# Transposing through a DMA copy, as one-pass float32r, in a four-layer decoder trunk

## The chip, the cores and the metric

The kernel runs on one core of a Trainium2 chip. The metric is device time in microseconds (us) from start to end of one execution. The compute engines of a core have queues of their own and run side by side: PE (TensorE) does matrix products and transposes into PSUM, ACT (ScalarE) and DVE (VectorE) do elementwise work, POOL (GpSimd) does some elementwise work too and can issue DMAs, SP (SyncE) only issues DMAs. A profile of one execution lists the instructions of each engine, PE's loads of its stationary operand in a row of their own (PEld).

## The reference

One sequence of 256 tokens of width 1024 goes through four pre-norm residual layers, all in float32. Each layer has a token mixer (layers 0 and 3 stick-breaking attention with 8 heads, layer 1 differential attention, layer 2 a short gated convolution), a cross-attention into 256 memory tokens, an output projection, and a SwiGLU feed-forward layer with inner width 2816:

```python
mem_n = _rmsnorm(mem, g_mem)
for i in range(DEPTH):
    kind = i % N_MIXERS
    hn = _rmsnorm(x, g_mix[i])
    proj = hn @ w_in[i]                       # 1024 -> 3 * 1024 + 256
    cols, mq = proj[..., :3 * MIX_WIDTH], proj[..., 3 * MIX_WIDTH:]
    if kind == 0:
        mix = _stick_breaking(cols)
    elif kind == 1:
        mix = _diff_attention(cols, lam_q1[j], ...)
    else:
        mix = _short_conv(cols, conv_w[j])    # gate_b * conv3(gate_c * h)
    mo = _memory_attention(mq, mem_n, w_mem_kv[i])
    x = x + jnp.concatenate([mix, mo], axis=-1) @ w_o[i]
    x = x + _swiglu(_rmsnorm(x, g_ffn[i]), w_ffn_in[i], w_ffn_out[i])
return _rmsnorm(x, g_final)
```

## The kernel before

**Weights.** The weights stream from HBM once. `wchunk` loads 512 KB (two blocks of 128 input channels by 512 columns, or one by 1024) into one of three `raw` buffers over SP's queue and splits it exactly in two: ACT writes the leading part `whi` (line 128), DVE the remainder `wlo` (line 129), both float32r, from a pool `wsplit` with eight buffers for each. Activations are split in the same way, and `mm3` (lines 133 to 135) makes each product of three float32r products: high by high, high by low, low by high. There are 428 chunks and 1728 such triples.

**Projections.** `proj` multiplies the 256 tokens, as two tiles of 128 (index `t`), by 512 columns: for each tile 8 blocks of input channels, so 24 products into one PSUM bank, and then an evacuation by ACT or DVE (`evac`). All four chunks of a projection are used by tile 0 and then again by tile 1, so a chunk becomes free only in the second tile. The first projection of the kernel loads one block a chunk, eight chunks in all. `out_proj` accumulates four PSUM banks at once over all chunks of a matrix.

**Transposes.** A projection's result has tokens on the partitions; attention, the convolution and the next product need channels there. So the evacuated tile is transposed on PE, 128 by 128 at a time, against a float32 identity `ident`, into PSUM, and copied or split from there. Queries, keys and the two convolution operands go through `to_T` (line 260), the product of the SwiGLU gate and its partner (tile `sg`, made by lines 742 and 744) through `hidden` (line 750). Normed activations (line 248), memory queries and keys, attention weights and head outputs are transposed elsewhere, by lines that the change leaves alone.

**Order.** On PE the instructions stand in the order in which the program emits them. A transposition must wait for ACT's or DVE's evacuation, so it is emitted later: `later(n, f)` puts `f` on a list, and each `flush` lowers the counts and emits what has come to zero. `proj` calls `flush` after half of a tile's products and at its end, before the tile's own evacuation is emitted; `out_proj` calls it after each chunk. One round is thus 12 products of 512 columns. With `later(1, ...)` the transposes of tile 0 come in the middle of tile 1, and those of tile 1 in the middle of the next projection's tile 0. The attention scores of a group of heads come a round after its last key transposes (`later(2, scores)`), and the following steps are chained by further rounds. ACT, DVE and POOL queues are ordered by a planner that follows the data and the free buffers.

Line numbers are those of this kernel; the changed functions and their callers:

Of the kernel before, what the change touches and what calls it, by code (L numbers as in the profile page):

```python
# [17 lines left out]
P = 128  # L18
# [12 lines left out]
QSCALE = 128.0 ** -0.5  # L31
NEG = -1e30

# columns of the per-channel vectors, one column per chunk of 128 channels
V_MIX, V_FFN, V_MEM, V_HEAD, V_CONV = 0, 32, 64, 72, 74
NV = 98

# [2 lines left out]
def trunk_kernel(ctx, tc, x, mem, vecs, w_in, w_kv, w_o, w_f1, w_f2, lams, g_final, out):  # L40
# [1 line left out]
    pool = lambda name, bufs, **k: ctx.enter_context(tc.tile_pool(name=name, bufs=bufs, **k))  # L42
    const = pool("const", 1)
    wraw = pool("wraw", 3)
    wsplit = pool("wsplit", 8)
    big = pool("big", 12)
    xtp = pool("xtp", 2)
    work = pool("work", 2)
# [3 lines left out]

    nc.scalar.preload_act_table_set("natural_log_exp_and_others")

    # products that nothing reads bring the tensor engine to its full clock while the first loads run
    warm = work.tile([P, 512], BF16, name="warm", tag="mk")
    nc.vector.memset(warm, 0.0)

# [4 lines left out]

    warm_up(6)

# [1 line left out]
    xs = []  # L67
    vec = const.tile([P, NV], F32, name="vec")

# [9 lines left out]

    ident = const.tile([P, P], F32, name="ident")  # L80
    make_identity(nc, ident)
    nhalf = const.tile([P, 8], F32, name="nhalf")
    nc.gpsimd.memset(nhalf, -0.5)
    tmp = work.tile([P, 3, P], F32, name="tmp", tag="att", bufs=6)[:, 0, :]
# [6 lines left out]
    nc.vector.tensor_copy(ntri, tmp)  # L91

    def strictly_causal(blocks):
        """[key, query] blocks k0q0, k0q1, k1q1: zero where key >= query"""
        diag = blocks[:, 0::2, :]
        nc.gpsimd.affine_select(out=diag, in_=diag, compare_op=ALU.is_gt, fill=0.0, base=0,
                                pattern=[[0, 2], [1, P]], channel_multiplier=-1)

    def alibi(hh0):
        """ALiBi bias with the causal mask, two heads, in [query, key] blocks (q0k0, q1k0, q1k1)"""  # L100
        dist = work.tile([P, 3, P], F32, name="dist", tag="att", bufs=6)
        for blk, base in ((0, 0), (1, P), (2, 0)):
            nc.gpsimd.iota(dist[:, blk, :], pattern=[[-1, P]], base=base, channel_multiplier=1,
                           allow_small_or_imprecise_dtypes=True)
        ab = big.tile([P, 2, 3, P], F32, name="abias", tag="big")
        for e in range(2):
            nc.gpsimd.tensor_scalar(ab[:, e], dist, -(2.0 ** (-2.0 * (hh0 + e + 1))), None, ALU.mult)
            for blk in (0, 2):
                nc.gpsimd.affine_select(out=ab[:, e, blk, :], in_=ab[:, e, blk, :], compare_op=ALU.is_ge,
                                        fill=NEG, base=0, pattern=[[-1, P]], channel_multiplier=1)  # L110
        return ab

# [1 line left out]
    wlast = []  # L114

    def wchunk(srcs, nk, ncol, ahead=False):
# [17 lines left out]
        nc.tensor.matmul(ps, lh, wl, start=False, stop=False)  # L134
        return nc.tensor.matmul(ps, ll, wh, start=False, stop=last)  # L135

    # work that waits for other engines is emitted some rounds of products later
    pend = []

    def later(rounds, f):  # L140
# [11 lines left out]
            flush()  # L152

    def proj(cols, xT, evac, start=None):
        """xT.T @ (columns of a weight matrix); evac(t, psum)"""
        ncol = sum(s.shape[1] for s in cols)
        nk = 1 if start else 2 if ncol == 512 else 4
        ch = []

        def load(c):  # L160
            ch.append(wchunk([s[c:c + nk * P, :] for s in cols], nk, ncol, start is not None))

        def mms(ps, t, kc):
            hi, lo = ch[kc // nk]
            return mm3(ps[:, :ncol], xT[t][0][:, kc, :], xT[t][1][:, kc, :], hi[:, kc % nk, :],
                       lo[:, kc % nk, :], kc == 0, kc == NKD - 1)

        ps = None
        done = 0
        if start:  # L170
            ps = ps_acc.tile([P, 512], F32, name="acc", tag="acc")
            done = 3
            with tc.issue_after(head[0][1]):
                load(0)
            with tc.issue_after(head[1][0]), tc.issue_after(head[1][1]):
                for kc in range(1, done):
                    load(kc * P)
            for kc in range(done):
                last = mms(ps, 0, kc)
            start(last.ins)  # L180
        for c in range(done * P, D, nk * P):
            load(c)
        for t in range(NT):
            if ps is None:
                ps = ps_acc.tile([P, 512], F32, name="acc", tag="acc")
            for kc in range(done, NKD):
                mms(ps, t, kc)
                if kc == 3 and ncol == 512:
                    flush()
            flush()  # L190
            evac(t, ps)
            ps, done = None, 0

    def out_proj(w, order, lhs, lag, evac, settle=None):
        """lhs.T @ w over the chunk pairs in `order`; the halves of token tile 0 end first"""
        acc = [[ps_acc.tile([P, 512], F32, name="acc", tag="acc") for _ in range(2)] for _ in range(NT)]
        chunks = [2 * kp + k for kp in order for k in range(2)]
        n = len(chunks)

        def mms(t, h, j, ch):  # L200
            lh, ll = lhs(chunks[j], t)
            sl = slice(h * 512, (h + 1) * 512)
            mm3(acc[t][h], lh, ll, ch[0][:, 0, sl], ch[1][:, 0, sl], j == 0, j == n - 1)

        tail = []
        for j, kc in enumerate(chunks):
            ch = wchunk([w[kc * P:(kc + 1) * P, :]], 1, D)
            if j < n - 2 * lag:
                for t in range(NT):
                    for h in range(2):  # L210
                        mms(t, h, j, ch)
                flush()
            else:
                tail.append((j, ch))
        if settle is not None:
            settle()
        for t in range(NT):
            for h in range(2):
                for j, ch in tail:
                    mms(t, h, j, ch)  # L220
                flush()
                evac(t, h, acc[t][h])

# [1 line left out]
    def rstd_of(ss, n, scale, eps):  # L225
        """(ss * scale + eps) ** -0.5"""
        r = small.tile([P, n], F32, name="rstd", tag=f"rstd{n}")
        nc.gpsimd.tensor_scalar(r, ss, scale, eps, ALU.mult, ALU.add)  # L228
        nc.gpsimd.tensor_tensor(r, r, nhalf[:, :n], ALU.pow)
        return r  # L230
# [9 lines left out]
                xtp.tile([P, NKD, P], F32R, name="xtl", tag="xtl"))  # L240

    def transposed(dst, src, gcol, h):
        """half h of (src * g).T in two parts of 12 bits: [channel, chunk, token]"""
        th, tl = dst
        ps = ps_x.tile([P, 4, P], F32, name="tr", tag="tr")
        for c in range(4):
# [7 lines left out]
                nc.vector.tensor_tensor(tl[:, sl, :], xg, th[:, sl, :].bitcast(F32), ALU.subtract).ins, last_pe)  # L254

    def to_T(src, dst, eng):
        """[token, 512] -> dst [512 as (128, 4), token]"""
        ps = ps_x.tile([P, 4, P], F32, name="tr", tag="tr")
        for c in range(4):
            nc.tensor.transpose(ps[:, c, :], src[:, c * P:(c + 1) * P], ident)  # L260
        if eng == 0:
            nc.scalar.copy(dst, ps)
        else:
            nc.vector.tensor_copy(dst, ps)

# [1 line left out]
    memT, mem_r = [], []  # L267

    def split(dst, src, t):
        """dst [channel, (hi, lo), chunk, token]"""  # L270
        hi, lo = (dst[:, j, :, t * P:(t + 1) * P] for j in range(2))
        nc.scalar.copy(hi, src)
        nc.vector.tensor_tensor(lo, src, hi.bitcast(F32), ALU.subtract)
# [18 lines left out]
        return kT, vn  # L292

    def mem_attention(qT, kv):
        """-> [channel of 2 heads, (hi, lo), pair, token]"""
        kT, vn = kv
        o = big.tile([P, 2, 2, S], F32R, name="om", tag="big")
        pTs = [big.tile([P, 2, NT, S], F32, name="mpT", tag="big") for _ in range(2)]
# [58 lines left out]
        first()  # L357
        return o

# [1 line left out]
    def qkv_evac(dst, scale):  # L361
        def evac(t, ps):
            n = work.tile([P, 512], F32, name="qkn", tag="qkn", bufs=4)
            nc.scalar.activation(n, ps, AF.Copy, scale=scale[t])
            later(1, lambda: to_T(n, dst[:, :, t * P:(t + 1) * P], 1))
        return evac

    def sb_scores(qT, kT, a, then):
# [166 lines left out]
            nc.sync.dma_start(out[t * P:(t + 1) * P, 512:], xs[t][:, 512:])  # L535
        return evac

# [1 line left out]
    xT, rx = [], []  # L539

    def first_norm(t):
# [48 lines left out]
        return lam, ghead  # L590


# [1 line left out]
    kv = None  # L594
    for i in range(DEPTH):
        kind = i % 3
# [37 lines left out]
        if kind != 2:  # L634
            v = [big.tile([P, D], F32, name=f"v{t}", tag="big") for t in range(NT)]

            def mixer(g):
# [28 lines left out]
                proj(col(D + g * 512), xT, qkv_evac(kT, rx))  # L666
                if i == 0 and g == 0:
                    load_mem()
                later(2, scores)
                proj(col(2 * D + g * 512), xT, v_evac)  # L670
        else:
            def mixer(g):
# [6 lines left out]

                def h_evac(t, ps):  # L680
                    nc.vector.scalar_tensor_tensor(cn[t], ps, rx[t], cn[t], ALU.mult, ALU.mult)
                    later(1, lambda: to_T(cn[t], uT[:, :, t * P:(t + 1) * P], 1))

                def mix():
                    outputs(g)
# [4 lines left out]
                    memory()  # L690
                proj(col(2 * D + g * 512), xT, h_evac)
                proj(col(g * 512), xT, qkv_evac(bT, rx))
                later(2, mix)

        mixer(0)
        if i == 0:
# [26 lines left out]
        out_proj(w_o[i], [4, 0, 1, 2, 3], o_lhs, 2, residual(V_FFN + 8 * i, nxt, rnx), drain)  # L723
        xT, rx = nxt, rnx

# [1 line left out]
        hts = []  # L727
        for b in range(6):
            n = 512 if b < 5 else 256
# [9 lines left out]
            def h_out(t, g_ps, u_ps, hh=hh, hl=hl, sg=sg, n=n):  # L739
# [2 lines left out]
                    nc.scalar.activation(s, g_ps, AF.Silu, scale=rx[t])  # L742
                if u_ps is not None:
                    nc.vector.scalar_tensor_tensor(s, u_ps, rx[t], s, ALU.mult, ALU.mult)  # L744
                    later(1, lambda: hidden(t, s, hh, hl, n))

            def hidden(t, s, hh, hl, n):
                tr = ps_x.tile([P, 4, P], F32, name="tr", tag="tr")
                for c in range(n // P):
                    nc.tensor.transpose(tr[:, c, :], s[:, c * P:(c + 1) * P], ident)  # L750
                src = tr[:, :n // P, :]
                hi = hh[:, :, t * P:(t + 1) * P]
                nc.scalar.copy(hi, src)
# [49 lines left out]
```

## Time and profile before

| what | value |
|---|---|
| runs without the profiler | 1305.54, 1305.54 and 1306.93 us, median 1305.54 |
| profiled execution, first to last instruction | 1308.2 us |
| mean granted TensorE clock | 0.997 |
| PE busy | 1293.7 us, 99% |
| PE weight loads | 1070.8 us, 82% |
| DVE, ACT, POOL busy | 762.8, 672.4, 51.4 us |
| DMA queue of SP | 226.31 MB, 56.7% of 16 engines' time |

The profile gives no other time for its execution than the span, which is 2.7 us above the median. A row for a group of instructions reads: line, engine, operation, out<-in by the program's names, shapes, count | busy us, mean ns of one | idle time of the engine before them and what ended it. A row of the timeline reads: start in us, duration in us, engine, line, operation, tiles, shapes, count. PE's instructions overlap in a pipeline, so the pace of a stretch is read from the starts, not from the durations. For PE's `tr<-ident,sg` and the like, the two operands stand in alphabetical order.

### The profile page before, as it was taken

What the parts mean: (1) busy time and instruction counts of PE and PEld (TensorE: products, weight loads), DVE (VectorE), ACT (ScalarE), POOL (GpSimd) and SP (SyncE); (2) the same over time, 40 slices, a digit from 0 to 9 for tenths busy, and PEclk for the clock granted to TensorE, in tenths of its full rate; (3) what the DMA queues carried; (4) which work ended last, traced back from release to release, by engine and by line L of the source; (5) the groups of instructions that cost most, each with busy time, mean ns of one, the idle gap of its engine ahead of it and who ended that gap; (6) DMA issues with size and microseconds to landing.
All of it is one profiled execution on the core that took longest, in us unless ns stands there. A gap on an engine that the chain in (4) does not pass through costs nothing.

```text
span 1308.2 us, 16273 instructions
## 1 busy us (share of the span) xinstructions
PE 1293.7 (99%) x6175; PEld 1070.8 (82%) x6175; DVE 762.8 (58%) x955; ACT 672.4 (51%) x943; POOL 51.4 (4%) x109
## 2 busy tenths in 40 slices
PE   9899999999999999999999999999999999999997
PEld 6788888888888888888888888888888888888886
DVE  6665565554567656555456775555546655655542
ACT  5766455444455545444445545444435655554441
POOL 0100000000011000000000000000000001000001
PEclk9999999999999999999999999999999999999999
DMA  7644566657554456665655565655665445656561
GB/s 228 208 141 149 161 181 185 181 179 218 154 173 136 146 161 194 193 185 182 199 158 175 157 188 175 186 181 185 206 192 174 130 129 162 183 185 182 183 220 45
DMA packets 107790, 227.34 MB, mean 174 GB/s; under 512 B 7488, under 2 KB 20288, under 8 KB 107712
## 3 DMA queue, kind: packets, MB, share of 16 engines
q1 hardware_dynamic: 107712, 226.31, 56.7%
q8 instruction: 48, 0.79, 0.2%
q14 instruction: 30, 0.25, 0.1%
HBM read 225.23 MB, written 1.05 MB: 173 GB/s over the span
## 4 chain that ended last, share of the span: by engine, by line
PE 93%; DMA 2%; DVE 2%; ACT 1%; issue 0%; POOL 0%; SPq 0%; POOLq 0%; ACTq 0%; DVEq 0%
PE acc L133 28%; PE acc L135 28%; PE acc L134 28%; PE tr L750 1%; DMA raw<-in_w_in 1%; PE tr L248 1%; PE tr L260 1%; PE at L308 1%; DVE wlo L129 1%; PE at L339 1%; DMA memn<-in_mem 1%; PE at L373 1%; PE tr L326 1%; DMA raw<-in_w_o 1%; PE at L415 1%
## 5 line engine op out<-in xcount | busy, mean ns | idle before, releaser
L129 DVE TENSOR_TENSOR wlo<-raw,whi 128x1024 fp32r<-128x1024 f32 (+1 forms) x428 | 518.5, 1215 | 391.4 <-ACT whi L128 382.2
L128 ACT CAST whi<-raw 128x1024 fp32r<-128x1024 f32 (+1 forms) x428 | 444.5, 1044 | 412.1 <-PE acc L135 255.9
L133 PE MATMUL acc<-whi,xth 128*128 128x512 f32 (+1 forms) x1152 | 454.3, 395 | 0.1
L134 PE MATMUL acc<-wlo,xth 128*128 128x512 f32 (+1 forms) x1152 | 442.7, 384 | 1.5 <-DVE wlo L129 1.5
L135 PE MATMUL acc<-whi,xtl 128*128 128x512 f32 (+1 forms) x1152 | 443.6, 385 | 0.0
L135 PEld LDWEIGHTS acc<-whi,xtl 128*128 128x128 f32 x1152 | 216.6, 188 | 43.9
L134 PEld LDWEIGHTS acc<-wlo,xth 128*128 128x128 f32 x1152 | 217.2, 189 | 42.3 <-DVE wlo L129 2.7
L133 PEld LDWEIGHTS acc<-whi,xth 128*128 128x128 f32 x1152 | 216.7, 188 | 41.2 <-issue 0.8
L133 PE MATMUL acc<-whi,hh 128*128 128x512 f32 x320 | 125.4, 392 | 0.0
L135 PE MATMUL acc<-whi,hl 128*128 128x512 f32 x320 | 124.6, 389 | 0.0
L134 PE MATMUL acc<-wlo,hh 128*128 128x512 f32 x320 | 124.6, 389 | 0.0
L135 PEld LDWEIGHTS acc<-whi,hl 128*128 128x128 f32 x320 | 60.1, 188 | 12.5
L134 PEld LDWEIGHTS acc<-wlo,hh 128*128 128x128 f32 x320 | 60.1, 188 | 12.2
L133 PEld LDWEIGHTS acc<-whi,hh 128*128 128x128 f32 x320 | 60.1, 188 | 12.2
L742 ACT ACTIVATE sg<-acc,rstd 128x512 f32<-128x512 f32 (+1 forms) x48 | 31.4, 654 | 49.5 <-PE acc L135 49.5
L133 PE MATMUL acc<-whi,oh 128*128 128x512 f32 x128 | 51.1, 399 | 0.0
L744 DVE SCALAR_TENSOR_TENSOR sg<-acc,rstd,sg 128x512 f32<-128x512 f32 (+1 forms) x48 | 33.8, 704 | 28.4 <-PE acc L135 20.5
L135 PE MATMUL acc<-whi,ol 128*128 128x512 f32 x128 | 50.0, 391 | 0.0
L134 PE MATMUL acc<-wlo,oh 128*128 128x512 f32 x128 | 49.9, 390 | 0.0
L235 ACT ACTIVATE junk<-x 128x1024 bf16<-128x1024 f32 x16 | 16.9, 1058 | 36.8 <-DVE x L714 36.5
L228 POOL TENSOR_SCALAR rstd<-ss 128x1 f32<-128x1 f32 x16 | 5.4, 336 | 642.9 <-ACT junk L235 642.8
L714 DVE TENSOR_TENSOR x<-acc,x 128x512 f32<-128x512 f32 x28 | 19.3, 688 | 18.9 <-PE acc L135 18.4
(185 smaller groups left out, 1080.3 us busy)
## 6 DMA issues: line engine op xcount, KB each, us to landing
raw<-in_w_ffn_in SPq DMA_DIRECT2D x160, 512.0 KB, 4.3
raw<-in_w_in SPq DMA_DIRECT2D x100, 512.0 KB, 4.4
raw<-in_w_ffn_out SPq DMA_DIRECT2D x88, 512.0 KB, 4.2
raw<-in_w_o SPq DMA_DIRECT2D x40, 512.0 KB, 4.4
raw<-in_w_mem_kv SPq DMA_DIRECT2D x16, 512.0 KB, 4.6
raw<-in_w_ffn_in SPq DMA_DIRECT2D x32, 256.0 KB, 3.7
raw<-in_w_in SPq DMA_DIRECT2D x8, 256.0 KB, 5.8
x<-in_x SPq DMA_DIRECT2D x4, 256.0 KB, 4.2
```

The costliest lines, as they stand in the source:

```text
L128: nc.scalar.copy(hi, raw)
L129: wlast[:] = [nc.vector.tensor_tensor(lo, raw, hi.bitcast(F32), ALU.subtract)]
L133: nc.tensor.matmul(ps, lh, wh, start=first, stop=False)
L134: nc.tensor.matmul(ps, lh, wl, start=False, stop=False)
L135: return nc.tensor.matmul(ps, ll, wh, start=False, stop=last)
L235: nc.scalar.activation(junk, src, AF.Square, accum_out=ss)
L248: last_pe = nc.tensor.transpose(ps[:, c, :], src[:, kc * P:(kc + 1) * P], ident).ins
L260: nc.tensor.transpose(ps[:, c, :], src[:, c * P:(c + 1) * P], ident)
L308: nc.tensor.matmul(ps[:, pr, :], qT[r * 64:(r + 1) * 64, a, pr, t * P:(t + 1) * P], kT[r * 64:(r + 1) * 64, b, pr, :], start=a + b == 0, s ...
L714: nc.vector.tensor_tensor(xs[t][:, sl], acc, xs[t][:, sl], ALU.add)
L742: nc.scalar.activation(s, g_ps, AF.Silu, scale=rx[t])
L744: nc.vector.scalar_tensor_tensor(s, u_ps, rx[t], s, ALU.mult, ALU.mult)
```

## The change

The 80 transposed tiles of `to_T` and `hidden` are copied first, by a DMA issued from POOL's queue, from SBUF to a second SBUF tile `bits` (four buffers of 128 by 512 float32). The transposes read this copy, and input, identity and output are named float32r in place of float32. They are emitted two rounds after the evacuation instead of one, and what comes after them, the scores and the convolution, three instead of two. To make room, `wsplit` has seven buffers instead of eight for each half. Nothing else changes but comments.

```diff
-    wsplit = pool("wsplit", 8)
+    wsplit = pool("wsplit", 7)
...
     ident = const.tile([P, P], F32, name="ident")
     make_identity(nc, ident)
+    ident_r = const.tile([P, P], F32R, name="ident_r")
+    nc.vector.tensor_copy(ident_r, ident)
+
+    def passed_on(src):
+        dst = work.tile([P, 512], F32, name="bits", tag="bits", bufs=4)[:, :src.shape[1]]
+        nc.gpsimd.dma_start(dst, src)
+        return dst
+
+    def turned(dst, src):
+        nc.tensor.transpose(dst.bitcast(F32R), src.bitcast(F32R), ident_r)
...
     def to_T(src, dst, eng):
         ps = ps_x.tile([P, 4, P], F32, name="tr", tag="tr")
         for c in range(4):
-            nc.tensor.transpose(ps[:, c, :], src[:, c * P:(c + 1) * P], ident)
+            turned(ps[:, c, :], src[:, c * P:(c + 1) * P])
...
             nc.scalar.activation(n, ps, AF.Copy, scale=scale[t])
-            later(1, lambda: to_T(n, dst[:, :, t * P:(t + 1) * P], 1))
+            bits = passed_on(n)
+            later(2, lambda: to_T(bits, dst[:, :, t * P:(t + 1) * P], 1))
...
-                later(2, scores)
+                later(3, scores)
...
                     nc.vector.scalar_tensor_tensor(cn[t], ps, rx[t], cn[t], ALU.mult, ALU.mult)
-                    later(1, lambda: to_T(cn[t], uT[:, :, t * P:(t + 1) * P], 1))
+                    bits = passed_on(cn[t])
+                    later(2, lambda: to_T(bits, uT[:, :, t * P:(t + 1) * P], 1))
...
-                later(2, mix)
+                later(3, mix)
...
                     nc.vector.scalar_tensor_tensor(s, u_ps, rx[t], s, ALU.mult, ALU.mult)
-                    later(1, lambda: hidden(t, s, hh, hl, n))
+                    bits = passed_on(s)
+                    later(2, lambda: hidden(t, bits, hh, hl, n))
...
                 for c in range(n // P):
-                    nc.tensor.transpose(tr[:, c, :], s[:, c * P:(c + 1) * P], ident)
+                    turned(tr[:, c, :], s[:, c * P:(c + 1) * P])
```

## The prediction

> **What bounds the kernel now.** I read the page from its top, then PE's waits, then PE's timeline around one transposed tile.
>
> ```profile
> span 1308.2 us, 16273 instructions
> PE 1293.7 (99%) x6175; PEld 1070.8 (82%) x6175; DVE 762.8 (58%) x955; ACT 672.4 (51%) x943; POOL 51.4 (4%) x109
> ...
> PE 93%; DMA 2%; DVE 2%; ACT 1%; issue 0%; POOL 0%; SPq 0%; POOLq 0%; ACTq 0%; DVEq 0%
> ```
>
> ```profile
> PE tr L248 <- DMA memn<-in_mem: 3.8, 1, 3.8
> PE acc L134 <- DVE wlo L129: 1.5, 3, 0.8
> PE warm_ps L62 <- DVE warm L57: 1.2, 1, 1.2
> PE tr L326 <- ACT qkn L364: 0.6, 1, 0.6
> PE tr L491 <- DVE df_o L483: 0.2, 1, 0.2
> ```
>
> PE carries 93% of the chain that ended last, and all its waits (total us, times, longest) come to 7.3 us. So nearly every nanosecond that PE's stream loses or gains is in the span, and a wait put into that stream is paid in full. What the changed transposes take there is read from starts, since the instructions overlap:
>
> ```profile
> 889.13 0.39 PE L133 MATMUL acc<-whi,xth 128*128 128x512 f32 x1
> 889.35 0.39 PE L134 MATMUL acc<-wlo,xth 128*128 128x512 f32 x1
> 889.58 0.39 PE L135 MATMUL acc<-whi,xtl 128*128 128x512 f32 x1
> 889.81 0.60 PE L750 MATMUL tr<-ident,sg 128*128 128x128 f32 x4
> 890.17 0.48 PE L133 MATMUL acc<-whi,xth 128*128 128x512 f32 x1
> 890.48 0.40 PE L134 MATMUL acc<-wlo,xth 128*128 128x512 f32 x1
> 890.72 0.40 PE L135 MATMUL acc<-whi,xtl 128*128 128x512 f32 x1
> ```
>
> Two plain products pass between 889.13 and 889.58: 0.225 us each. From L135 to the next L135, 889.58 to 890.72, it is 1.14 us for three products and four transposes; 1.14 - 3 x 0.225 = 0.465 us for the four. Inside the group the pace is (0.60 - 0.27) / 3 = 0.11 us a transpose, 0.27 being the duration of the last:
>
> ```profile
> L750 PE MATMUL tr<-ident,sg 128*128 128x128 f32 x176 | 26.9, 271 | 0.0
> L260 PE MATMUL tr<-ident,qkn 128*128 128x128 f32 x112 | 17.1, 275 | 0.0
> L374 PE MATMUL at<-qT,kT 128*128 128x128 f32 x32 | 6.0, 274 | 0.0
> L391 PE MATMUL at<-sb_uh,nones 128*128 128x128 f32 x16 | 3.6, 222 | 0.0
> L260 PE MATMUL tr<-ident,cn 128*128 128x128 f32 x16 | 2.4, 271 | 0.0
> ```
>
> 176 + 112 + 16 = 304 transposes change: 72 groups of four and 8 of two (the last, 256 wide block of each feed-forward layer has two tiles). At 0.465 and about half of that they hold 33.5 + 1.9 = 35 us, 2.7% of the span. This is all there is to win.
>
> **One pass instead of two.** Compare float32 and float32r over the same 128 columns: L374 (float32) lasts 274 ns, L391 (float32r) 222. The transposes, at 271 to 275, look like the float32 one. A pass less is 52 ns, so the product's pace would be 0.11 - 0.05 = 0.06 us. The products are not alone: each transpose loads its own stationary operand, and only one load runs ahead. PE's load row tells how fast loads can follow each other where the product beside them has one pass:
>
> ```profile
> 1055.81 0.19 PEld L390 LDWEIGHTS at<-sb_ul,ntri 128*128 128x128 f32 x1
> 1055.92 0.19 PEld L391 LDWEIGHTS at<-sb_ul,nones 128*128 128x128 f32 x1
> ...
> 1056.10 0.14 PEld L260 LDWEIGHTS tr<-ident,qkn 128*128 128x128 f32 x1
> 1056.16 0.14 PEld L260 LDWEIGHTS tr<-ident,qkn 128*128 128x128 f32 x1
> ```
>
> After a plain float32r load the next starts 0.11 us later, after a transposing load 0.06. The transposing load is also recorded as shorter: 0.14 against 0.19, which both plain types have (L374 is float32, L391 float32r):
>
> ```profile
> L374 PEld LDWEIGHTS at<-qT,kT 128*128 128x128 f32 x32 | 5.9, 190 | 0.9
> ...
> L391 PEld LDWEIGHTS at<-sb_ul,nones 128*128 128x128 f32 x16 | 3.1, 191 | 0.0
> ```
>
> No float32r transpose stands in this trace, so its load may be like either. At 0.06, three of the four steps of a group shrink by 0.052; the fourth does not, as the next product's own load (L133, a plain one, 0.11) starts with it. That is 72 x 0.156 + 8 x 0.052 = 11.6 us. At 0.11 nothing is won; if the fourth step shrank too it would be 72 x 0.208 + 8 x 0.104 = 15.8. Below nothing is excluded: neither row is slower than today's 0.11. I take 11.6: as plain loads of the two types last the same, it is the transposing form and not the type that makes a load short.
>
> The Trainium skill, "TensorE: Matmul & The Clock Gate", section "LDWEIGHTS (loading the stationary operand)", speaks against this: a load takes its columns over 1.2 GHz, an estimated 107 ns for 128 columns, whatever the operand. The plain loads above agree; the transposing load, at 0.06, does not. By that rule the sum would be a gain of nothing.
>
> **The copies.** 80 DMAs are added to POOL's queue, 72 of 256 KB and 8 of 128. PE now waits for a copy. What it may take follows from when the copy can start and when PE comes to it:
>
> ```profile
> 910.02 0.75 DVE L744 SCALAR_TENSOR_TENSOR sg<-acc,rstd,sg 128x512 f32<-128x512 f32 x1 [1.00 <-PE acc L135]
> ...
> 916.79 0.74 DVE L744 SCALAR_TENSOR_TENSOR sg<-acc,rstd,sg 128x512 f32<-128x512 f32 x1
> ```
>
> ```profile
> 912.54 0.60 PE L750 MATMUL tr<-ident,sg 128*128 128x128 f32 x4
> ...
> 918.47 0.60 PE L750 MATMUL tr<-ident,sg 128*128 128x128 f32 x4
> ```
>
> From group to group are 24 products and one group: 5.93 - 0.465 = 5.46 us, so the extra round of 12 products moves each group 2.73 us later. For tile 0 the evacuation ends at 910.77 and the group would come at 915.27: 4.5 us. For tile 1 DVE is held by a weight split and ends at 917.53, the group would come at 921.2: 3.67 us. The 24 feed-forward pairs all have this form. The 32 groups of line 260 follow an evacuation by ACT or, for four of them, by DVE; where the tile is taken up at once they have tile 0's 4.5 us. The least has the very first, where ACT is still in a weight split:
>
> ```profile
> 18.15 0.68 ACT L364 ACTIVATE qkn<-acc,rq 128x512 f32<-128x512 f32 x1
> ```
>
> ```profile
> 19.08 0.60 PE L260 MATMUL tr<-ident,qkn 128*128 128x128 f32 x4
> ```
>
> 19.08 + 2.73 - 18.83 = 2.98 us. How long a copy takes from issue to landing no row shows; the nearest ones move the same 256 KB over SP's queue:
>
> ```profile
> q1 hardware_dynamic: 107712, 226.31, 56.7%
> ...
> raw<-in_w_ffn_in SPq DMA_DIRECT2D x32, 256.0 KB, 3.7
> raw<-in_w_in SPq DMA_DIRECT2D x8, 256.0 KB, 5.8
> ...
> out<-x SPq DMA_DIRECT2D x4, 256.0 KB, 2.2
> ```
>
> At the end of the kernel, out of SBUF and with nothing beside it, 2.2 us; with the weight stream beside it, 3.7, or 5.8 where it queued. The copies share the engines with that stream but not its queue, so I take 3.7. Then each tile 1 is late by 0.03 us (24 x 0.03 = 0.7), the group at 19.08 by 0.7, and I allow one more like it: 2 us in all for waits. At 2.2 it is nothing. At 5.8 tile 0 waits 1.3 us, and tile 1 the 0.83 that remain after that wait: 24 x 2.13 = 51 us, and some 20 more for line 260.
>
> The net is a gain of 11.6 - 2 = 9.6 us. The break-even landing is 3.67 + 11.6 / 24 = 4.15, and a little less, 4.05, with the other groups.
>
> **Parts costed at nothing.** The copies add 19.9 MB to 226.31, some 5 points to the 56.7% of DMA time. POOL is 4% busy; behind a copy that waits for its evacuation stand the masks of the stick-breaking weights, for which ACT and then PE wait, and the norms' `rstd`, for which the evacuations wait; these are rounds of 2.7 us away. On PE everything stands behind a waiting transpose. The evacuations from PSUM keep type and size. The scores start a round later; in layer 3 this moves the last head's values to just before the output projection's tail, where the heads before it (line 415) are left as cover; without it, 1 to 2 us. The eighth chunk of the first projection must wait until tile 1 has used the first one; tile 1's products cover its split, which without cover is about 2.3 us. With seven buffers a chunk is split when the chunk seven before it is free, so at the time at which its successor is split now. The tightest case is just after an output projection:
>
> ```profile
> 490.19 1.23 DVE L129 TENSOR_TENSOR wlo<-raw,whi 128x1024 fp32r<-128x1024 f32 x1 [0.97 <-ACT whi L128]
> ```
>
> ```profile
> 495.94 0.39 PE L133 MATMUL acc<-whi,xth 128*128 128x512 f32 x1
> ```
>
> The split that ends at 491.42 is that of the chunk after the one whose first product starts at 495.94: 4.5 us of lead are left, so nothing waits. If one split more came between, 1.2 us of that would go.
>
> **The rivals.** *The copies are late (slower than before).* DMAs issued from POOL need POOL's own work, and POOL is held up by DVE:
>
> ```profile
> L96 POOL TENSOR_SCALAR_AFFINE_SELECT sb_p<-sb_p x16: 408/540/1069, 59.6 to 1099.1; 128x256 f32<-128x256 f32 x16
> ```
>
> The same mask takes 408 ns, or up to 1069 where DVE runs its weight split (line 129) beside it. If a copy's issue is held like that, 0.66 us longer, it lands after 4.36: 24 x 0.69 = 17 us for the second tiles and some 4 for the rest. Net 21 - 11.6 = 9 us slower, 1315. It decides from a landing of about 4.3 on (4.05 plus what a measurement can tell). Against it: the mask reads SBUF, an issue only names addresses.
>
> The Trainium skill, "SBUF — State Buffer", section "Who interferes with whom", has this as a rule: a DVE instruction with two SBUF inputs blocks a GpSimd instruction that reads SBUF. The L96 rows agree; it adds that descriptor writing is spared by such DVE instructions (an inference there), which no run here shows.
>
> *The load stays at 0.11 (it does not do what it says).* Then no pass saved is seen: 1305.5 + 2 = 1307.5 with copies that land after 3.7, more with later ones. For it: every float32r load in the trace takes 0.11. Against it: the float32 ones outside transposes do too, by the L374 row.
>
> *A queue is reordered.* The planner places copies, splits and masks anew; one of them behind a copy that waits would hold ACT or DVE. At about 1.2 us (one split) for each of the 8 changes between projection and feed-forward, 1306. Nothing in the profile speaks for it but that all queues are planned together.
>
> **How the numbers follow.** Forecast 0.47, late copies 0.25, plain load 0.20, reordered 0.08. 1308.2 - 9.6 = 1298.6 for the profiled execution, which lies 2.7 above the median of the runs; carried over to the median, 1305.5 - 9.6 = 1296. The forecast's own range is 1292 (a landing under 3.6, a little of the fourth step) to 1302. For eight in ten I go up through the late copies at 1315 to 1318, a landing of 4.45. What a measurement of this kernel can tell is about 0.2%, 2.6 us. Faster: the forecast and little else, 0.48. Same: three quarters of the plain load and part of the reordering, 0.21. Slower: late copies, and plain load with late copies, 0.31.
>
> **What would show it.** The changed L750 and L260 rows near 222 ns, and groups of four that take 0.31 instead of 0.465 us; transposing loads 0.06 apart. If these are still 0.11 apart, the plain load was right. The copies' median from issue to landing, against 3.67 and 4.5. PE's waits naming the DMA of `bits`, some 2 us in total; 10 or more is the first rival. PE waiting for `wlo` after the first 20 us would show that seven buffers are too few.

## The result, and the profile after

The changed kernel takes 1352.6 us (median of four runs, 1348.75 to 1354.0) against 1305.78 before: ratio 1.0344, 95% interval 1.0329 to 1.0358. It is slower by 3.4%, where 1296 had been forecast. The profiled execution has a span of 1346.8 us against 1308.2, which is 38.6 us more. The medians differ by 46.8, since this execution of after was the fastest of its four and that of before lay above its median; what follows accounts for the 38.6. All medians are of executions in the fast state; one execution of the last kernel below took 3868 us and is left out.

The page of after from its top, PE's waits (us in total, times, longest), and the rows that answer to those of the transposes and the DMAs:

```profile
span 1346.8 us, 16633 instructions
```

```profile
PE tr L93 <- DMA bits<-sg: 26.8, 25, 3.0
PE tr L93 <- DMA bits<-qkn: 7.9, 7, 1.3
...
PE acc L147 <- DVE wlo L142: 1.1, 2, 0.8
...
PE tr L93 <- DMA bits<-cn: 0.6, 1, 0.6
```

```profile
q1 hardware_dynamic: 107712, 226.31, 54.8%
q0 software_dynamic: 6144, 19.93, 3.7%
...
PE 48%; issue 37%; DMA 7%; ACT 3%; POOL 2%; DVE 2%; SPq 0%; POOLq 0%; ACTq 0%; DVEq 0%
...
L93 PE MATMUL tr<-ident_r,bits 128*128 128x128 f32 x304 | 38.3, 247 | 35.5 <-DMA bits<-sg 26.8
...
bits<-sg POOLq DMA_DIRECT2D x40, 256.0 KB, 4.2
...
bits<-qkn POOLq DMA_DIRECT2D x28, 256.0 KB, 4.7
```

All 304 transposes now stand on one line, L93. PE waits 35.3 us for their copies in 33 waits. The wait for `wlo` is as small as before, so the seven buffers starve nothing. The chain of waits misleads here: it gives PE only 48% and 37% to "issue". From a late copy it goes back along POOL's queue and counts that queue's idle time between two copies as "issue" (17.2 us from 551.11 to 568.35, for example), although PE works all the while. The view of PE's waits, which sums all of them, is the one to read.

Which copies are late shows in one pair, the two token tiles of one block of the inner layer. First POOL's timeline, then PE's around the two groups:

```profile
615.85 0.55 POOL L88 DMA_DIRECT2D bits<-sg  x1 [17.10 <-DVE sg L759]
622.15 0.55 POOL L88 DMA_DIRECT2D bits<-sg  x1 [5.76 <-DVE sg L759]
```

```profile
619.82 0.39 PE L148 MATMUL acc<-whi,xtl 128*128 128x512 f32 x1
620.05 0.46 PE L93 MATMUL tr<-ident_r,bits 128*128 128x128 f32 x4
620.34 0.47 PE L146 MATMUL acc<-whi,xth 128*128 128x512 f32 x1
620.65 0.39 PE L147 MATMUL acc<-wlo,xth 128*128 128x512 f32 x1
620.88 0.40 PE L148 MATMUL acc<-whi,xtl 128*128 128x512 f32 x1
```

```profile
625.66 0.39 PE L148 MATMUL acc<-whi,xtl 128*128 128x512 f32 x1
627.41 0.51 PE L93 MATMUL tr<-ident_r,bits 128*128 128x128 f32 x4 [1.36 <-DMA bits<-sg]
627.76 0.46 PE L146 MATMUL acc<-whi,xth 128*128 128x512 f32 x1
628.06 0.39 PE L147 MATMUL acc<-wlo,xth 128*128 128x512 f32 x1
628.29 0.40 PE L148 MATMUL acc<-whi,xtl 128*128 128x512 f32 x1
```

The first tile's copy landed 2.65 us after its issue (the trace has the landing of each), and its group came at 620.05, straight behind the product before it. The second tile's landed after 5.13, and PE stood for 1.36 us. Both issues lasted 0.55 us on POOL; nothing held them. What differed was the DMA engines. Their queues in the two stretches, 615.9 to 618.5 and 622.2 to 627.3 (packets, MB, share of 16 engines):

```profile
q1 hardware_dynamic: 119, 0.42, 39.9%
q0 software_dynamic: 80, 0.26, 25.4%
```

```profile
q1 hardware_dynamic: 289, 1.05, 66.4%
q0 software_dynamic: 80, 0.26, 12.7%
```

The copy is the same 80 packets and holds the engines equally long, 0.254 x 2.6 = 0.66 us and 0.127 x 5.1 = 0.65. It does not move more slowly; its packets stand between those of q1, the weight loads. In the trace the first packet of the second copy starts 2.0 us after the issue instead of 1.2, the last 4.8 us instead of 2.3. Over all copies of after, by tile and by how many weight loads were in flight between 0.8 and 2.3 us after the issue, which is when a quiet copy moves:

| copies | number | landing, median us |
|---|---|---|
| inner layer, first tile / second tile | 24 / 24 | 2.61 / 4.76 |
| queries, keys, convolution `bT`, first / second | 14 / 14 | 2.35 / 4.86 |
| no load in flight | 6 | 2.29 |
| one | 28 | 2.47 (1.97 to 4.88) |
| two | 22 | 4.65 |
| three | 24 | 4.80 |

Together, 36 of the 80 groups come 41.1 us later than straight behind the product before them, 29.0 of that in the 24 second tiles of the inner layer.

One more piece is at the end of the kernel. The last rows of the chain of before, of after, and of a later experiment (copies issued from ACT, one round more):

```profile
1302.97 0.59 POOLq L799
1303.59 0.75 DVE x L534
```

```profile
1338.80 0.59 POOLq L815
1339.42 0.75 DVE x L548
```

```profile
1292.60 0.59 POOLq L815
1293.21 0.75 DVE x L548
```

From the end of that DVE row to the end of the span it is 1308.2 - 1304.34 = 3.9 us before, 1346.8 - 1340.17 = 6.6 after, and 1297.8 - 1293.96 = 3.8 in the experiment. The POOLq row is the instruction that closes POOL's queue. Its full length in the trace:

```
before                        1302.97 to 1303.62
after                         1338.80 to 1346.01
from ACT, one round more      1292.60 to 1293.26
```

With copies on POOL's queue the closing takes 7.2 us instead of 0.65 and outlasts the output's landing (1342.87) by 3.1; it adds 2.8 us to the span. So far 41.1 + 2.8. Against it stands what the float32r transposes give: the group at 620.05 takes 620.88 - 619.82 - 3 x 0.225 = 0.385 us where before took 0.465. In a late group less is left: from 625.66 to the next L148, which starts at 628.29, it is 2.63 - 0.675 - 1.52 of lateness = 0.435. With 0.08 us for each of the 40 wide groups that come on time, 0.025 for four narrow ones and 0.03 for the 36 late ones this gives 4.4 us. 41.1 + 2.8 - 4.4 = 39.5, for the measured 38.6.

That this comes so close is in part luck, since two more things differ. PE's other waits fell from 7.3 to 4.5 us, most of it in the one for `memn` (3.8 and 1.0). And the granted clock was not full all the time. The longest wait for a copy comes near the end:

```profile
1275.91 0.39 PE L148 MATMUL acc<-whi,hl 128*128 128x512 f32 x1
1279.29 0.50 PE L93 MATMUL tr<-ident_r,bits 128*128 128x128 f32 x2 [2.99 <-DMA bits<-sg]
...
1280.57 0.63 PE L148 MATMUL acc<-whi,hl 128*128 128x512 f32 x1
1280.99 0.63 PE L146 MATMUL acc<-whi,hh 128*128 128x512 f32 x1
```

From 1278.64 on the clock was granted at 0.5 for 6.83 us, and the products start 0.43 us apart instead of 0.225; up to 1285.59 some 2.8 us are lost. In the kernel before, 3.41 us at 0.5 follow the `memn` wait, which costs up to 1.7. In the traces of this case each of the six PE waits longer than 2.8 us has such a stretch in it or within 1 us behind it. With both, 39.5 - 2.8 + 1.1 = 37.8, and 0.8 us stay open.

### The profile page after: what moved, and what is told of

Its sections match the earlier page's. It is cut to its first block, busy times and chain, and to the rows that moved or that the text cites. A ratio compares the mean times of both kernels' runs of the same rounds, so it can differ in the third digit from the quotient of the medians.

```text
span 1346.8 us, 16633 instructions
## 1 busy us (share of the span) xinstructions
PE 1296.6 (96%) x6175; PEld 1063.9 (79%) x6175; DVE 763.4 (57%) x956; ACT 675.2 (50%) x943; POOL 98.8 (7%) x189
## 4 chain that ended last, share of the span: by engine, by line
PE 48%; issue 37%; DMA 7%; ACT 3%; POOL 2%; DVE 2%; SPq 0%; POOLq 0%; ACTq 0%; DVEq 0%
PE acc L146 14%; PE acc L148 14%; PE acc L147 14%; DMA bits<-sg 3%; DMA bits<-qkn 2%; POOL bits L88 2%; DMA raw<-in_w_in 1%; DVE wlo L142 1%; ACT whi L141 1%; PE tr L93 1%; PE at L321 1%; PE tr L261 1%; PE at L352 1%; ACT junk L248 1%; PE tr L339 1%
## 5 line engine op out<-in xcount | busy, mean ns | idle before, releaser
L148 PE MATMUL acc<-whi,xtl 128*128 128x512 f32 (+1 forms) x1152 | 443.1, 385 | 0.0
L148 PEld LDWEIGHTS acc<-whi,xtl 128*128 128x128 f32 x1152 | 216.4, 188 | 43.5
L148 PE MATMUL acc<-whi,hl 128*128 128x512 f32 x320 | 125.6, 392 | 0.0
L93 PEld LDWEIGHTS tr<-ident_r,bits 128*128 128x128 f32 x304 | 32.4, 141 | 55.1 <-issue 22.0
L93 PE MATMUL tr<-ident_r,bits 128*128 128x128 f32 x304 | 38.3, 247 | 35.5 <-DMA bits<-sg 26.8
L148 PEld LDWEIGHTS acc<-whi,hl 128*128 128x128 f32 x320 | 60.7, 190 | 12.9
L770 DVE TENSOR_TENSOR hl<-tr,hh 128x512 fp32r<-128x512 f32 x40 | 27.5, 686 | 62.6 <-ACT hh L769 62.6
L88 POOL DMA_DIRECT2D bits<-sg x48 | 26.2, 546 | 492.0 <-DVE sg L759 462.7
L148 PE MATMUL acc<-whi,ol 128*128 128x512 f32 x128 | 50.1, 391 | 0.0
```

The lines of the kernel that those rows point to most:

```text
L88: nc.gpsimd.dma_start(dst, src)
L93: nc.tensor.transpose(dst.bitcast(F32R), src.bitcast(F32R), ident_r)
L770: nc.vector.tensor_tensor(hl[:, :, t * P:(t + 1) * P], src, hi.bitcast(F32), ALU.subtract)
```

## The experiments

The theory after this reading: the loss is second tiles' copies that land late because weight loads are in flight beside them; the one-pass transposes are worth some 5 us, not 11.6. The rivals: seven buffers; POOL's issue, or DVE holding it; the float32r transposes themselves.

**Seven buffers alone.**

```diff
-    wsplit = pool("wsplit", 8)
+    wsplit = pool("wsplit", 7)
```

> The kernel before with seven instead of eight buffers for split weights, nothing else. Theory (the loss is PE waiting for copies that land late, the buffers cost nothing): within 1.5 us of the kernel before, 1304 to 1307.5, and no PE wait for wlo after the first 20 us. Rival (seven buffers starve the weight products): slower than 1310, with waits for wlo spread over the span.

1308.64 us against 1306.51 (ratio 1.001, 1.0001 to 1.002), 1.1 us above the theory's range and short of the rival's. The 2.1 us are less than the 0.2% that the prediction gave as what can be told here; PE's waits for `wlo` are 1.1 us, all in the first 11 us, as in after. The buffers are not the cause of a loss of 46.8.

**Copies that nobody reads.**

```diff
+            passed_on(n)
             later(1, lambda: to_T(n, dst[:, :, t * P:(t + 1) * P], 1))
```

The same ahead of the convolution's and the inner layer's `later(1, ...)`, with seven buffers.

> The kernel before with seven buffers, and with the 80 copies issued as in the changed kernel, but read by nobody: the transposes stay float32, read the evacuated tile itself and come as early as before. Theory (a copy costs only where PE waits for it): 1304 to 1309, as PE waits for no copy; the copies of the second token tiles still land after 4.4 us or more, those of the first after 2.6. Rival (the copies slow the weight stream, or hold POOL so that masks and norms come late): over 1315 even though nobody reads them.

1314.49 us, ratio 1.0051 (1.0039 to 1.0064): over the theory's range and just under the rival's, so a miss for both. The landings are those of after (inner layer 2.92 and 4.81, the others 2.60 and 4.88) although PE waits for none of them: lateness belongs to the copies, not to PE's wait. The 5.9 us above the kernel with seven buffers were not expected. 2.8 of them are the closing of POOL's queue (1305.29 to 1312.49 here). The rest can be looked for in the profiled executions, 1313.3 us against 1306.4 with seven buffers alone. PE's waits are 8.9 us in all against 7.1, the largest in the first loads:

```profile
PE tr L253 <- DMA memn<-in_mem: 3.8, 1, 3.8
PE acc L139 <- DVE wlo L134: 1.9, 3, 0.8
```

With seven buffers alone these are 1.8 and 1.1. And from 39.85 on, at the end of the `memn` wait, the clock was granted at 0.5 for 6.83 us, where the other profile has 3.41 us of that, at 10.77: up to 1.7 us more. Together 2.8 + 1.8 + 1.7 = 6.3 of the 6.9. Whether the copies bring this about is not shown: the `memn` wait was 3.8 us in the kernel before too, with 3.41 us at 0.5 behind it.

**Float32 transposes with the copies.**

```diff
-        nc.tensor.transpose(dst.bitcast(F32R), src.bitcast(F32R), ident_r)
+        nc.tensor.transpose(dst, src, ident)
```

> The changed kernel with its copies and rounds, but the transposes are float32 again (two passes). Theory (the copies cause the loss, the float32r transposes give back a few us): slower than the changed kernel by about 0.075 us for each of the 48 groups that come on time and little for the late ones, whose wait shrinks by as much: 1352.6 + 3.6 = 1356, 1353 to 1360. Rival (the float32r transposes themselves hold PE up): under 1335.

1356.79 us (1351.36 to 1359.88), ratio 1.0372 (1.0344 to 1.0401), where 1356 was expected. The loss is there without a single float32r transpose; that rival is out.

**Float32r transposes without the copies.** ACT and DVE write the evacuated tile as float32r.

```diff
-            nc.scalar.activation(n, ps, AF.Copy, scale=scale[t])
-            bits = passed_on(n)
-            later(2, lambda: to_T(bits, dst[:, :, t * P:(t + 1) * P], 1))
+            bits = rounded()
+            nc.scalar.activation(bits, ps, AF.Copy, scale=scale[t])
+            later(1, lambda: to_T(bits, dst[:, :, t * P:(t + 1) * P], 1))
```

`rounded()` is a float32r tile from the four buffers of `bits`; the other two evacuations likewise, scores and convolution after two rounds again.

> Float32r transposes without a copy: ACT and DVE write the evacuated tile as float32r, so that the low bits of queries, keys, convolution inputs and the inner layer are left out of the computation; rounds as in the kernel before, seven buffers. It measures what the one-pass transposes are worth alone. Theory (a group of four goes from 0.467 to 0.39 us, as the groups that came on time in the changed kernel): 72 x 0.077 + 8 x 0.03 = 5.8 us less than before, 1300, 1298 to 1302. The prediction's own size (steps of 0.06 us): 11.6 us less, 1294. Rival (a float32r transpose gains nothing, or costs): 1305 or more.

1301.08 us, ratio 0.9953 (0.9942 to 0.9965): 5.4 us faster than the 1306.51 beside it. The gain is real and half of what was predicted.

**One round more.**

```diff
-            later(2, lambda: to_T(bits, dst[:, :, t * P:(t + 1) * P], 1))
+            later(3, lambda: to_T(bits, dst[:, :, t * P:(t + 1) * P], 1))
...
-                later(3, scores)
+                later(4, scores)
```

The same for the convolution and the inner layer.

> The changed kernel with one round more: transposes three rounds after the evacuation instead of two, scores and convolution four instead of three. Theory (the loss is late copies alone): the second tiles' copies are due after about 6.4 us instead of 3.67, and landed by 5.9 at most but for the last one; waits for copies fall from 35 us to under 3, and the gain of the transposes is left, less up to 2 us where scores come later at the end of a layer: 1302, 1299 to 1306. Rival (POOL, the queues' order or the DMA engines hold up other work as well): over 1320, with waits that name something else than bits.

1306.67 us, ratio 0.9995 (0.9986 to 1.0003): the whole loss is gone, with copies that land as late as ever (inner layer 2.59 and 4.78). PE's waits:

```profile
PE acc L147 <- DVE wlo L142: 2.9, 4, 1.7
...
PE tr L93 <- DMA bits<-qkn: 1.2, 1, 1.2
```

It is 0.7 us over the theory's range. 2.8 us are the closing of POOL's queue.

**Copies issued from ACT.**

```diff
-        nc.gpsimd.dma_start(dst, src)
+        nc.scalar.dma_start(dst, src)
```

> The changed kernel with its 80 copies issued from ACT's queue instead of POOL's. Theory (the DMA engines are shared with the weight stream's burst): it matters little who issues; second tiles land after 3.7 us or more, waits for bits of 15 us or more, 1330 to 1356. Rival (POOL's way of issuing, which needs POOL's own work, makes them late): second tiles land after 2.2 to 3 us, waits below 4 us, 1299 to 1306.

1350.66 us, ratio 1.0324 (1.0296 to 1.0351). The copies now lie in another queue and are issued 0.03 us after the evacuation instead of 0.30, and still the second tiles of the inner layer land after 5.11 us (first 3.14), and PE waits:

```profile
PE tr L93 <- DMA bits<-sg: 31.4, 26, 4.3
PE tr L93 <- DMA bits<-qkn: 4.2, 6, 1.5
...
PE tr L93 <- DMA bits<-cn: 0.9, 1, 0.9
```

Who issues does not matter for the landing. The Trainium skill, "SBUF — State Buffer", section "SBUF: two separate sides", says that while DVE runs an instruction in a two-port mode, a DMA issued from GpSimd can look blocked because its descriptors cannot be written, and that a DMA from ACT's queue then runs at full speed. The runs here show no such thing for these copies: from ACT they land no earlier. The Trainium skill, "DMA: Bandwidth & Descriptors", section "Queues, rings and completion order", has each DMA engine serve its queues in turn, a packet at a time; that agrees with a copy whose packets lie between those of the weight loads.

**Half, and a quarter, of the weight loads.** Two (or up to four) successive chunks of one form are split out of the same loaded tile; copies on POOL and rounds are those of after. The products use wrong weights for the chunks that are not loaded.

```diff
+        elif kept and list(kept[0].shape) == [P, nk, ncol]:
+            raw = kept.pop()
+            srcs = []
         else:
             raw = wraw.tile([P, nk, ncol], F32, name="raw", tag="raw")
+            kept[:] = [raw]
```

> The changed kernel with every second weight load left out: two successive chunks are split out of the same loaded tile, so the products use wrong weights for half of the chunks, while splits, products, copies and rounds all stay. Theory (second tiles' copies are late because they share the DMA engines with a burst of weight loads): the second tiles' copies land after 2.3 to 3.5 us, waits for bits fall below 8 us, 1300 to 1312. Rival (they are late because POOL's issue or descriptor work is held by DVE's splits, which are all still there): second tiles still land after 4.4 us or more, waits of 30 us or more, 1345 to 1355.

> The changed kernel with three of four weight loads left out: up to four successive chunks of one form are split out of the same loaded tile, so the products use wrong weights for most chunks; splits, products, POOL's copies and rounds stay. Theory (a copy is late where weight loads are in flight beside it): second tiles' copies of the inner layer land after 2.3 to 3.2 us, those of queries and keys, where no load is issued beside them, too; waits for bits below 3 us in all; 1302 to 1308, with the closing of POOL's queue (2.8 us) still in it. Rival (DVE's splits or POOL's own work delay them): second tiles' medians stay at 3.5 and 4.7 us as with half of the loads.

With half of the loads 1309.05 us (ratio 1.0013, 1.0004 to 1.0023), with a quarter 1302.79 (0.9963, 0.995 to 0.9976). The rows of the copies, first with half, then with a quarter:

```profile
bits<-sg POOLq DMA_DIRECT2D x40, 256.0 KB, 3.1
...
bits<-qkn POOLq DMA_DIRECT2D x28, 256.0 KB, 3.4
```

```profile
bits<-sg POOLq DMA_DIRECT2D x40, 256.0 KB, 2.3
bits<-qkn POOLq DMA_DIRECT2D x28, 256.0 KB, 2.3
```

Second tiles of the inner layer: 4.76, 3.55 and 2.29 us with all, half and a quarter of the loads. PE's waits for `bits`: 35.3, 4.8 and none that the view lists. DVE's splits, POOL's issues, the products and the transposes are the same in all three, so the loads are the cause. One expectation missed: with half of the loads the second tiles of queries and keys still landed after 4.75, and the inner layer's 3.55 is just over the 3.5 expected. The late ones are copies that still met a load at the same moment. Four of them were issued at 104.38, 362.93, 418.13 and 429.77 us, and weight loads at 104.42, 362.87, 417.81 and 429.82; they landed after 4.5 to 5.3. Where the load was issued 0.93 us before the copy, as for most second tiles of the inner layer, they landed after 3.3 to 4.0. With a quarter of the loads the second tiles of queries and keys land after 2.44 in the median. One 512 KB load issued at the same moment is enough to double a copy's landing.

**What a transpose costs in the steady state.** Each group issued twice over, so that it has eight (the narrow ones four): once in the kernel before, once in the version with ACT's queue and one round more.

```diff
-        for c in range(4):
+        for c in (0, 1, 2, 3) * 2:
```

> The same kernel (copies from ACT's queue, one round more) with each group of float32r transposes issued twice over into the same tile, so that a group has eight (the narrow ones four): what four more cost is their steady pace. Theory (0.086 us a transpose, which was the last step of the groups): 72 x 0.344 + 8 x 0.172 = 26 us above the same kernel with single groups, 1326.5, 1323 to 1329. The prediction's pace (0.06 us): 18 us, 1318.7. A plain load's pace (0.11): 33 us, 1334.

> The kernel before with each group of float32 transposes issued twice over. It gives the steady pace of the two-pass transposes for comparison. Theory (0.109 us): 72 x 0.436 + 8 x 0.218 = 33 us above the kernel before, 1339.6, 1336 to 1342. If the float32 group's pace is also set by something at its borders alone: under 1330.

Float32r: 1325.39 us, 24.8 above the 1300.62 of single groups, 24.8 / 304 = 0.082 us each. Float32: 1338.71, 31.4 above the 1307.31 of before, 0.103 each. PE and its loads in one group of eight, float32r first:

```profile
611.19 0.39 PE L148 MATMUL acc<-whi,xtl 128*128 128x512 f32 x1
611.41 0.80 PE L93 MATMUL tr<-ident_r,bits 128*128 128x128 f32 x8
612.05 0.46 PE L146 MATMUL acc<-whi,xth 128*128 128x512 f32 x1
```

```profile
613.57 0.39 PE L135 MATMUL acc<-whi,xtl 128*128 128x512 f32 x1
613.80 1.03 PE L750 MATMUL tr<-ident,sg 128*128 128x128 f32 x8
614.59 0.48 PE L133 MATMUL acc<-whi,xth 128*128 128x512 f32 x1
```

The medians of the single steps, over 72 groups, from the trace (ns from start to start; the last is the step to the next weight product):

```
float32r  products  60  64  85  86  86  84  83  88
float32   products 109 109 109 109 109 109 109  28
float32r  loads     86  86  87  85  85  84
float32   loads    109 109 109 109 109 109
```

In float32 each product starts 107 ns behind its own load, which starts with the product before: the products pace the group, and the weight product comes 28 ns after the last. Their 109 ns are about twice the 56 that 128 columns take at the pace of the float32r weight products (225 for 512), which fits two passes. In float32r the loads pace the group: from the second on they start 85 ns apart, with each product 35 ns behind its load, and the next weight product comes only after 88.

**ACT's queue and one round more**, which puts the two edits above together:

```diff
-        nc.gpsimd.dma_start(dst, src)
+        nc.scalar.dma_start(dst, src)
...
-            later(2, lambda: to_T(bits, dst[:, :, t * P:(t + 1) * P], 1))
+            later(3, lambda: to_T(bits, dst[:, :, t * P:(t + 1) * P], 1))
```

> Copies issued from ACT's queue and one round more (transposes after three rounds, scores and convolution after four). Theory: as with the additional round alone, waits for bits under 3 us, 1299 to 1306; ACT's issues cost PE nothing. Rival (issues on ACT hold up evacuations and splits behind a copy that waits for DVE): over 1310, with PE waits for ACT or wlo.

> The kernel with copies issued from ACT's queue and one round more, once more and beside the kernel before in more rounds, since three runs gave 1300.5 against 1306.7. Theory (nothing waits for the copies, the transposes' gain of some 5.5 us is left): 1299 to 1303, an interval for the ratio wholly below 0.998. Rival (the earlier difference was that of a few runs): the interval reaches 0.999 or more.

1300.15 us (median of three; ratio 0.9942, 0.9921 to 0.9962), and once more 1300.62 (0.9949, 0.9937 to 0.9962): 0.5% faster than before, and faster than both kernels of this case, and nothing is left out of the computation. PE's waits and the row of the transposes in the second profile:

```profile
PE acc L147 <- DVE wlo L142: 1.9, 3, 0.8
...
PE tr L93 <- DMA bits<-qkn: 0.2, 1, 0.2
```

```profile
L93 PE MATMUL tr<-ident_r,bits 128*128 128x128 f32 x304 | 35.3, 237 | 0.2 <-DMA bits<-qkn 0.2
```

The second tiles of the inner layer still land after 5.04 us; the 6.7 us from evacuation to use (median of the wide blocks) cover that. Its time and that of the version without copies, 1301.08, agree: a copy that nobody waits for, issued from ACT, costs nothing that can be measured. Over one round more with POOL's copies (1306.67) it gains 6 us. Between the two profiled executions, 1304.8 and 1297.8 us, it is 7.0: 2.8 are the closing of the queue, and 4.1 are PE's waits of all kinds, 8.3 us against 4.2. Why these differ is open.

## Why the prediction was wrong, step by step

**What bounds the kernel.** Right: PE's stream is the span, and waits put into it were paid in full: 35 us of waits came out as a loss of that size.

**The landing of 3.7 us is the step that failed.** The prediction took one landing for all copies, from loads of the same size, against due times of 4.5 and 3.67 us. The due times were right or close: PE would have come to the groups of the wide blocks 4.49 and 4.04 us after the evacuation (medians), so in the inner layer 21 of 24 first tiles were on time and all 24 second tiles late. But the landing is not one number: 2.6 us for first tiles and 4.8 for second ones. "The copies share the engines with that stream but not its queue" treated the queue as the protection and the sharing as small; the runs show the sharing to be the price, and a queue of its own, POOL's or ACT's, not to protect a copy from it (copies in SP's own queue were not tried). The second tiles, for which the due time was the shorter, are also those issued while two or three weight loads are in flight. With the landing measured, the prediction's own formula gives 24 x (4.76 - 3.67) = 26 us for the measured 29.0, but that is near by luck: it left out 0.29 us from the evacuation's end to POOL's issue and 0.14 from the landing to the first transpose, and had the second due time 0.37 too short; 24 x (4.76 + 0.29 + 0.14 - 4.04) = 28. Its break-even of 4.05 to 4.15 was worked out with the gain of 11.6 and was not tested; the second tiles' landing is above it.

**The rival of late copies** had the mechanism on PE's side, and the sign, but the wrong cause and too small a size (1315). It had POOL's issue held by DVE; the issue lasted 0.54 us in the median whether DVE ran or not, and copies from ACT were as late. Of its price, the landing of 4.36 was taken for a slow issue; contention gives 4.76, and the range ended at 4.45.

**The gain of 11.6 us** was right in sign and half in size: 5.4 to 6.7 measured by two kernels that wait for nothing. The mis-sized term is the step of 0.06 us, taken from two loads that followed each other by 0.06 at the head of a group. That is what the first steps take (60, 64 ns); then loads pace the group at 85. And the fourth step, which the prediction let stand, grows from 28 to 86 ns. 49 + 45 + 24 - 58 = 60 ns a group from the steps of products, 80 with the weight products next to the group. The load's spacing of 0.085 lies between the two that the prediction weighed, so neither its forecast nor the rival of the plain load (0.11) was right. The Trainium skill's rule in "TensorE: Matmul & The Clock Gate", section "LDWEIGHTS (loading the stationary operand)", gives an estimated 107 ns for 128 columns: no run here shows a float32r transposing load that slow; in the long groups they stand 85 ns apart.

**The parts costed at nothing.** Seven buffers: right, by the run with seven alone. The DMA time of the copies (3.7% of the engines) was counted as 5 points of a 57% mean and so as harmless; a mean over the span says nothing of the moment at which a copy is issued. The round by which scores come later: no loss shows, even with two rounds. The masks and norms behind a waiting copy on POOL: PE's waits name none. Missing from the list was the closing of POOL's queue, 2.8 us. *A queue reordered*: nothing shows it.

## What to carry to other kernels

A transfer's landing is a property of the moment at which it is issued: read which loads are in flight just then, not the mean share of the DMA engines, and plan with the slow case (here 5 us for 256 KB beside the weight stream, 2.3 without). When a transfer is put between a producer and the bounding engine, give the consumer enough time for the slow case; here one round more turned 3.4% slower into no loss, and with the issue moved off POOL into 0.5% faster. A pace should be read from the steady part of a long group, and the step out of the group counted with it.

## What was not expected of the hardware

- Copies on POOL's queue lengthen the closing of that queue at the end of the program from 0.65 to 7.2 us, in all six traces that have them, whether or not they are read; 2.8 us of that lie behind everything else.
- A 256 KB copy inside SBUF lands after 2.3 us with quiet engines, and after 4.8 with two or more 512 KB loads in flight, though its own packets hold the engines for 0.65 us in both cases.
- A wait of 2.99 us at PE cost some 2.8 us more behind it, as the granted clock was 0.5 for 6.83 us and the products started 0.43 us apart instead of 0.225.
- A float32r transpose is paced by its load at 0.085 us where a float32 one takes 0.109, so that one pass instead of two gives 22%, not a half.
